# Modulations of a two-block network: fused multiply-and-sum on VectorE for all columns, none as products on TensorE

## The chip, the cores and the metric

The kernel runs on one core of a Trainium2 chip. The time is the device time of one execution in microseconds (us), lower is better. A core has TensorE (PE, the matrix engine, with its weight loads shown apart as PEld), VectorE (DVE), ScalarE (ACT), GpSimd (POOL, hardly used here) and SyncE (SP, which issues the DMAs here).

## What is computed

Two blocks are applied to 256 tokens of width 1024, in float32. The first is a recurrent mixer with a feed-forward; the second has two attention layers, which also carry 256 context tokens. Every layer of the second block is steered by modulations: six vectors of 1024 for the tokens, from a condition `c`, and six for the context, from `c_ctx`.

```python
def modulation(cond, w_ada, b_ada):
    m = jax.nn.silu(cond) @ w_ada + b_ada          # w_ada: [1024, 6144]
    return [t[..., None, :] for t in jnp.split(m, 6, axis=-1)]

def modulate(h, shift, scale):
    return h * (1 + scale) + shift

def second_block(x, c, ctx, c_ctx, w_ada, ...):
    for i in range(2):
        sh1, sc1, g1, sh2, sc2, g2 = modulation(c, w_ada[i], b_ada[i])
        csh1, csc1, cg1, csh2, csc2, cg2 = modulation(c_ctx, w_ada[i], b_ada[i])
        h = modulate(rms_norm(x, norm1_g[i]), sh1, sc1)
        ...                                        # projections, attention
        x = x + g1 * (mixed @ w_out[i])
        x = x + g2 * conv_ffn(modulate(rms_norm(x, norm2_g[i]), sh2, sc2), ...)
```

The modulations of a layer are thus two products of one row with a matrix of 1024 x 6144, and nothing of them depends on the tokens. They can be computed at any time before the layer's norms and residuals read them.

## The kernel before

Features lie on partitions, tokens along the free dimension. Every product is made from two float32r parts of each operand, a high one and a low one, in three passes (high x high, high x low, low x high; `mm3`, lines 404 to 407). A weight comes in tiles of 128 x 1024 (512 KB): `weight_raw` takes a buffer of the ring `raw` (4 buffers) and issues the DMA on SP's queue, `weight` lets ScalarE cast it to `wh` (line 383) and VectorE subtract that from the raw tile to give `wl` (line 385); both have 3 buffers. For 256 tokens one tile is 24 matmuls of 256 columns. 419 such tiles are used, besides those of the modulations. The matmuls of the last pass over a product wait for `wl`.

The program is written as Python generators, and a scheduler puts each engine's instructions into one fixed order when the kernel is compiled; an engine runs its list in that order, each instruction waiting for the semaphores it needs.

The modulations are filler work. `Ada.steps` is a generator; `ada_tick` is called after each weight tile and takes a step from it every `pace` ticks (`Knobs.pace0` to `pace3` for the stages), `ada_steps(n)` takes n steps, and `ada_rest` takes all that are left. Results go to `mods[layer]`, [128, 48, 2]: 48 blocks of 128 features for two conditions.

There are two forms of such a step:

- `ada_pe` (lines 523 to 558), on TensorE. 512 columns are four weight tiles, each cast and subtracted as any other, and per tile four matmuls of 512 columns with the conditions as the stationary operand (lines 541, 542). The sums stand on 4 partitions; two ScalarE copies, four transposes (line 528) and two VectorE sums bring them onto 128 partitions.
- `ada_dve` (lines 571 to 582), on VectorE. A transposed tile of 128 columns by 1024 rows, float32, goes through one fused instruction for each condition (line 580): multiply by the condition's row, sum along the free dimension, scale, add the bias. Such a step is one instruction and a short read of the accumulator. `ada_rows` (line 560) puts silu of the conditions on all partitions first (eight tanh, eight instructions of line 568). The tiles have a pool of their own, `araw`, with 3 buffers.

Layer 0's modulations are all made by `ada_pe(0)`, 48 tiles, from the first block's middle up to its feed-forward (called ffn1 below). Layer 1's first 5120 columns are made by `ada_dve(1)` in layer 0's feed-forward, 40 tiles and 80 steps, and the last 1024 by `ada_pe(1)`, 8 tiles, during layer 1's attention.

A feed-forward (`ffn`) runs over chunks of the hidden width: the up-projection (per hidden block two weights, a short convolution with four tap instructions on VectorE, SwiGLU, a split), then eight down products, each added to the residual stream `xres` on VectorE (line 1316 in ffn1, line 1641 in the second block). ffn1 has two such chunks, of 14 and 8 blocks. After the last one come the sums of squares (`sacc`, lines 471 and 473), a reduction of them on PE (`psn`), and the next norm; at the same time PE goes on with the next layer's first weights (`psx`, lines 429 to 431), which serve the context's tokens first.

Of the kernel before, what the change touches and what calls it, by code (L numbers as in the profile page):

```python
# [28 lines left out]
# columns of the modulations done on the tensor engine, 512 at a time, and on the vector engine, 128  # L29
ADA = ((range(0, 6144, 512), range(0)), (range(5120, 6144, 512), range(0, 5120, 128)))  # L30
# [3 lines left out]
# column offsets of the first block's w_in  # L34
# [4 lines left out]
# rows of the small projections: i gates, f gates, dt  # L39
# [3 lines left out]
def _ws(name, layer, c0, nk=8, r0=0):  # L43
    """[nk*128, 128] block of a weight, rows on partitions, 128 columns."""
    def cut(w):
        return w[name][layer][r0:r0 + nk * 128, c0:c0 + 128].reshape(nk, 128, 128).transpose(1, 0, 2)
    return nk * 128, cut


def _xs(name, layer, c0, half, cols=None):  # L50
    """[512, 256] block: rows on partitions, 256 columns that stream."""
    def cut(w):
        a = w[name][layer][half * 512:(half + 1) * 512]
        a = a[:, c0:c0 + 256] if cols is None else a[:, cols]
        return a.reshape(4, 128, 256).transpose(1, 0, 2)
    return 1024, cut


def _ada(layer, c0, q):
    """[256, 512] block: rows on partitions, 512 columns."""  # L60
    def cut(w):
        a = w["w_ada_2"][layer][q * 256:(q + 1) * 256, c0:c0 + 512]
        return a.reshape(2, 128, 512).transpose(1, 0, 2)
    return 1024, cut


def _adat(layer, c0):
    """[1024, 128] block: columns on partitions."""
    def cut(w):
        return w["w_ada_2"][layer][:, c0:c0 + 128].T  # L70
    return 1024, cut
# [16 lines left out]
def _qcols(c):  # L88
    """256 columns of the window attention's queries, heads j and j + 4 side by side."""
# [35 lines left out]
def plan2(layer):  # L125
    p = [(("ada", c0, q), _ada(layer, c0, q)) for c0 in ADA[layer][0] for q in range(4)]
    p += [(("adat", c0), _adat(layer, c0)) for c0 in ADA[layer][1]]
# [21 lines left out]
def _cols(v):  # L149
    """[n*128] -> [128, n]"""  # L150
    return v.reshape(-1, 128).T


def _convc(w):
    """[K, n*128] -> [128, n*K]"""
# [121 lines left out]
class Knobs:  # L277
# [4 lines left out]
    araw = 3  # L282
# [3 lines left out]
    pace3 = 5  # L286
# [3 lines left out]
    afill = tuple(range(20, 30))  # L290
# [9 lines left out]
def tile_two_blocks(ctx: ExitStack, tc: tile.TileContext, xT, ctxT, cst1, cst, cstw, pb1, pl0, pl1, pf0, pf1, pc, pcb, wb, w0, w1, out,  # L300
# [16 lines left out]
    class PS:  # L317
        """PSUM pools of the phase at hand"""

    def psum(**bufs):  # L320
        """Shares out the eight banks: name=number."""
# [7 lines left out]
    psum(g=3, s=4, a=1)  # L329
# [30 lines left out]
    ones = const.tile([128, 128], F32, name="ones")  # L360
    V.memset(ones, 1.0)
    onesn = const.tile([128, 128], F32, name="onesn")
# [5 lines left out]
    def bsel(r):  # L368
        """[128, 128]: row r ones; picks and broadcasts one row."""
        return ident[:, r:r + 1].to_broadcast([128, 128])  # L370

# [21 lines left out]
    def gained(dst_h, dst_l, x, g):  # L393
        """x g, split: what the first products after a norm take; 1 / rms is applied to their results"""
# [4 lines left out]
    def mm3(o, w, rhs, nk, late=False, first=True, last=True):  # L399
        """o = W^T x in three passes; late: the low part of x comes last."""  # L400
# [11 lines left out]
    def gemm_ws(ph, key, rhs, n, nk=8, late=False, w=None):  # L412
        """out[128 features, n tokens] = W^T x; rhs(k) gives (high, low)."""
# [6 lines left out]
    def gemm_xs(ph, keys, lhs, toks, evac):  # L420
        """out[128 tokens, 256 features]; lhs(k, t) gives (high, low) of a token tile."""
# [14 lines left out]
    def rsqrt_raw(pool, a, n, tag, bufs, rows=128):  # L436
        """RS * result = 1 / sqrt(a)"""
# [3 lines left out]
        # in two halves, so that neither waits for the step before  # L441
# [13 lines left out]
    def mean_sq(x, scale=None, eps=EPS):  # L455
        """mean of squares + eps, [128 tokens, 2 blocks of them], in PSUM"""
# [20 lines left out]
    def rms_all(a):  # L477
        """[128, 256] on every partition: 1 / (RS sqrt(a)) for tokens on partitions"""
# [19 lines left out]
    # =====================================================================  # L498
    # modulation: silu(c) w + b for both conditions, features on partitions
    # =====================================================================  # L500
    mods = [res.tile([128, 48, 2], F32, name="mod%d" % i) for i in range(2)]

    class Ada:
        pool = rows = None
# [5 lines left out]
    def ada_prep():  # L510
        zp = ctx.enter_context(tc.tile_pool(name="zp", bufs=1))
        Ada.cs = zp.tile([128, 8, 2], F32, name="ccs")
        Ada.cr = zp.tile([128, 8, 4], F32R, name="ccr")
        ct2 = zp.tile([128, 8, 2], F32, name="ct2")
        nc.sync.dma_start(out=ct2.rearrange("p k c -> p (k c)"), in_=pc)
        Ada.pf = [load_params(zp, _pf(i), (pf0, pf1)[i], "pf%d" % i) for i in range(2)]
        th = zp.tile([128, 8, 2], F32, name="cth")
        S.activation(out=th, in_=ct2, func=AF.Tanh, scale=0.5)
        V.scalar_tensor_tensor(th, th, 1.0, ct2, ALU.add, ALU.mult)
        V.tensor_scalar(Ada.cs, th, 0.5, None, ALU.mult)  # L520
        split(Ada.cr[:, :, 0:2], Ada.cr[:, :, 2:4], Ada.cs)

    def ada_pe(li):
        """512 columns at a time on the tensor engine; both parts of the conditions share a pass."""
        def finish(c0, rows):
            pt = PS.s.tile([128, 4, 4], F32, tag="s", name="psat")
            for q in range(4):
                T.transpose(pt[:, q], rows[q // 2][0:4, q % 2 * 128:q % 2 * 128 + 128], ident[0:4, 0:4])
            o = slice(c0 // 128, c0 // 128 + 4)
            V.tensor_tensor(mods[li][:, o], pt[:, :, 0:2],  # L530
                            Ada.pf[li]("bada")[:, o].unsqueeze(2).to_broadcast([128, 4, 2]), ALU.add)
            V.tensor_tensor(mods[li][:, o], mods[li][:, o], pt[:, :, 2:4], ALU.add)

        last = None
        for c0 in ADA[li][0]:
            ps = (PS.a or PS.s).tile([128, 512], F32, tag="s", name="psada")
            for q in range(4):
                wh, wl = weight(1 + li, ("ada", c0, q), 512)
                for kk in range(2):
                    k = 2 * q + kk  # L540
                    T.matmul(ps[0:4], Ada.cr[:, k], wh[:, kk], start=(k == 0), stop=False)
                    T.matmul(ps[0:2], Ada.cr[:, k, 0:2], wl[:, kk], start=False, stop=(k == 7))
                if last and q == 0:
                    finish(*last)
                if q < 3:
                    yield
            rows = [Ada.rows.tile([128, 256], F32, tag="arow", name="arow", bufs=2) if Ada.rows is not None else
                    tmp.tile([128, 256], F32, tag="t256", name="arow", bufs=6) for _ in range(2)]
            for e in range(2):
                S.copy(rows[e][0:4], ps[0:4, e * 256:(e + 1) * 256])  # L550
            last = (c0, rows)
            if Ada.rows is None:
                finish(*last)
                last = None
            yield
        if last:
            finish(*last)
            yield
# [1210 lines left out]
```

## Time and profile before

| | |
|---|---|
| median of 3 runs | 1763.69 us (1762.58 to 1768.16) |
| span of the profiled execution | 1767.7 us |
| PE busy | 1738.8 us, 98% |
| VectorE busy | 1384.8 us, 78% |
| ScalarE busy | 983.7 us, 56% |
| DMA | 276.97 MB, mean 157 GB/s |

The profile is that of one execution; its span is 4.0 us above the median of the runs. PE, VectorE and the others have one list of instructions each. A row's first time is its start, the second its length; an instruction may overlap the one before it on the same engine, so the cost of one in a row of them is read from start to start. "Idle before" is the time in which the engine stood still before an instruction, with what released it. The granted clock (PEclk) is the share of TensorE's full clock that it ran at.

### The profile page before, as it was taken

How to read it: one execution, taken by the hardware profiler on the slowest of the kernel's cores; microseconds unless marked ns; L12 is line 12 of the kernel's file. 1: busy time of each engine (PE TensorE's matmuls, PEld its weight loads, DVE VectorE, ACT ScalarE, POOL GpSimd, SP SyncE). 2: the span in 40 equal slices, each digit the busy share in tenths (PEclk: the TensorE clock that was granted, in tenths of full speed). 3: DMA queues.
4: the chain of work that ended last, by engine and by line, in shares of the span. 5: the costliest groups of instructions: out<-in, count | busy, mean ns of one | idle time of the engine just before them, and what ended most of it. 6: DMA issues, size and time to landing. Idle time of an engine off the chain costs nothing.

```text
span 1767.7 us, 31912 instructions
## 1 busy us (share of the span) xinstructions
PE 1738.8 (98%) x12442; PEld 1568.2 (89%) x12442; DVE 1384.8 (78%) x2716; ACT 983.7 (56%) x1723; POOL 0.2 (0%) x4
## 2 busy tenths in 40 slices
PE   7999999999999999999999999999999999999999
PEld 7999988878888999999878898888888997799999
DVE  7987967557778996877687799999656878788776
ACT  6655645445556865666676564442244556766554
POOL 0000000000000000000000000000000000000000
PEclk8999999999999999999989999999999999999999
DMA  7555445447677666654211356657433543046564
GB/s 233 159 154 152 138 132 157 147 126 222 218 228 228 187 190 221 209 170 139 86 67 47 105 163 189 183 171 232 129 96 107 168 132 120 24 141 195 174 196 132
DMA packets 80502, 276.97 MB, mean 157 GB/s; under 512 B 9056, under 2 KB 13792, under 8 KB 80224
## 3 DMA queue, kind: packets, MB, share of 16 engines
q1 hardware_dynamic: 80352, 274.94, 49.8%
q8 instruction: 98, 1.61, 0.4%
q14 instruction: 52, 0.43, 0.1%
HBM read 273.86 MB, written 1.05 MB: 156 GB/s over the span
## 4 chain that ended last, share of the span: by engine, by line
PE 51%; DVE 3%; ACT 1%; issue 0%; ACTq 0%
PE psg L404 12%; PE psg L407 12%; PE psg L406 11%; PE pso L1574 3%; PE psx L429 2%; PE psx L431 2%; PE psx L430 2%; PE psp L1562 2%; PE psc L1517 1%; PE psc L1519 1%; PE psc L1518 1%; DVE wl L385 0%; ACT Pp L1529 0%; DVE mx L1523 0%; PE psc L1521 0%
## 5 line engine op out<-in xcount | busy, mean ns | idle before, releaser
L383 ACT CAST wh<-raw 128x1024 fp32r<-128x1024 f32 (+1 forms) x475 | 490.9, 1037 | 531.0 <-PE psg L406 423.7
L385 DVE TENSOR_TENSOR wl<-raw,wh 128x1024 fp32r<-128x1024 f32 (+1 forms) x475 | 572.5, 1208 | 206.8 <-ACT wh L383 203.2
L404 PE MATMUL psg<-XH,wh 128*128 128x256 f32 (+1 forms) x1288 | 400.7, 314 | 3.6 <-ACT XH L390 1.9
L407 PE MATMUL psg<-XH,wl 128*128 128x256 f32 (+1 forms) x1288 | 398.8, 312 | 0.3 <-DVE wl L385 0.3
L406 PE MATMUL psg<-XL,wh 128*128 128x256 f32 (+1 forms) x1240 | 387.5, 313 | 0.7 <-DVE XL L1304 0.5
L404 PEld LDWEIGHTS psg<-XH,wh 128*128 128x128 f32 x1288 | 243.0, 189 | 22.0 <-ACT XH L390 2.3
L407 PEld LDWEIGHTS psg<-XH,wl 128*128 128x128 f32 x1288 | 243.3, 189 | 15.9 <-DVE wl L385 1.0
L406 PEld LDWEIGHTS psg<-XL,wh 128*128 128x128 f32 x1240 | 234.5, 189 | 16.1 <-DVE XL L1304 1.1
L404 PE MATMUL psg<-xh,wh 128*128 128x256 f32 x704 | 203.4, 289 | 1.8 <-ACT xh L390 1.3
L406 PE MATMUL psg<-xl,wh 128*128 128x256 f32 x704 | 200.5, 285 | 0.9 <-DVE xl L391 0.9
L407 PE MATMUL psg<-xh,wl 128*128 128x256 f32 x704 | 200.1, 284 | 0.3 <-DVE wl L385 0.3
L404 PE MATMUL psg<-hh,wh 128*128 128x256 f32 (+1 forms) x592 | 179.6, 305 | 0.1
L407 PE MATMUL psg<-hh,wl 128*128 128x256 f32 (+1 forms) x592 | 178.5, 302 | 0.0
L406 PE MATMUL psg<-hl,wh 128*128 128x256 f32 (+1 forms) x592 | 178.5, 302 | 0.0
L404 PEld LDWEIGHTS psg<-xh,wh 128*128 128x128 f32 x704 | 134.9, 192 | 6.0 <-ACT xh L390 1.5
L406 PEld LDWEIGHTS psg<-xl,wh 128*128 128x128 f32 x704 | 135.1, 192 | 2.9 <-DVE xl L391 1.4
L407 PEld LDWEIGHTS psg<-xh,wl 128*128 128x128 f32 x704 | 134.9, 192 | 2.2 <-issue 1.3
L406 PEld LDWEIGHTS psg<-hl,wh 128*128 128x128 f32 x592 | 111.5, 188 | 5.3 <-DVE hl L391 0.2
L404 PEld LDWEIGHTS psg<-hh,wh 128*128 128x128 f32 x592 | 110.9, 188 | 5.9 <-ACT hh L390 0.6
L407 PEld LDWEIGHTS psg<-hh,wl 128*128 128x128 f32 x592 | 111.2, 188 | 5.5
L429 PE MATMUL psx<-wh,XH 128*128 128x256 f32 x384 | 110.0, 287 | 1.1 <-DVE ss L1379 0.5
L430 PE MATMUL psx<-wh,XL 128*128 128x256 f32 x384 | 108.5, 283 | 0.0
(435 smaller groups left out, 3237.8 us busy)
## 6 DMA issues: line engine op xcount, KB each, us to landing
raw<-w SPq DMA_DIRECT2D x254, 512.0 KB, 3.7
raw<-wb SPq DMA_DIRECT2D x197, 512.0 KB, 4.3
araw<-w SPq DMA_DIRECT2D x40, 512.0 KB, 4.2
raw<-w SPq DMA_DIRECT2D x16, 384.0 KB, 3.4
raw<-wb SPq DMA_DIRECT2D x8, 384.0 KB, 3.2
xres<-xT SPq DMA_DIRECT2D x16, 128.0 KB, 3.6
plt<-pl SPq DMA_DIRECT2D x2, 588.0 KB, 5.5
xres<-ctxT SPq DMA_DIRECT2D x8, 128.0 KB, 2.7
```

Source lines behind the costliest of these rows:

```text
L383: S.copy(wh[:, 0:sz], raw[:, 0:sz])
L385: V.tensor_tensor(wl[:, 0:sz], raw[:, 0:sz], wh[:, 0:sz], ALU.subtract)
L404: T.matmul(o, wh[:, k], xh, start=(first and k == 0), stop=False)
L406: T.matmul(o, wh[:, k], xl, start=False, stop=False)
L407: T.matmul(o, wl[:, k], xh, start=False, stop=(last and not late and k == nk - 1))
L429: T.matmul(o, xh, wh[:, k % 4], start=(k == 0), stop=False)
L430: T.matmul(o, xl, wh[:, k % 4], start=False, stop=False)
L431: T.matmul(o, xh, wl[:, k % 4], start=False, stop=(k == 7))
L1517: T.matmul(o, qh, kh, start=True, stop=False)
L1518: T.matmul(o, qh, kl, start=False, stop=False)
L1562: T.transpose(ps[:, b], p[:, b * 128:(b + 1) * 128], ident)
L1574: T.matmul(po[:, i % 4], pt[:, b], v, start=(b == 0), stop=(b == nb - 1))
```

## The change

All 48 tiles of both layers become `ada_dve` steps, 96 for each layer; `ada_pe` goes, and with it the conditions' split, its small DMA, the transposes and the filler list `afill`.

```diff
-ADA = ((range(0, 6144, 512), range(0)), (range(5120, 6144, 512), range(0, 5120, 128)))
+ADA = range(0, 6144, 128)
...
-    p = [(("ada", c0, q), _ada(layer, c0, q)) for c0 in ADA[layer][0] for q in range(4)]
-    p += [(("adat", c0), _adat(layer, c0)) for c0 in ADA[layer][1]]
+    p = [(("adat", c0), _adat(layer, c0)) for c0 in ADA]
...
-    araw = 3
     pace0 = 1000
     pace1 = 2
     pace2 = 1
-    pace3 = 5
+    pace3 = 2
...
-    afill = tuple(range(20, 30))
...
-    psum(g=3, s=4, a=1)
+    psum(g=3, s=5)
...
     def ada_dve(li):
-        for c0 in ADA[li][1]:
-            o, sz = woff[1 + li][("adat", c0)]
+        for c0 in ADA:
             f = c0 // 128
-            raw = Ada.pool.tile([128, 1024], F32, tag="araw", name="araw", bufs=Knobs.araw)
-            nc.sync.dma_start(out=raw, in_=wsrc[1 + li][o:o + 128 * sz].rearrange("(p f) -> p f", p=128))
+            raw = weight_raw(1 + li, ("adat", c0))
             for c in range(2):
-                to = Ada.pool.tile([128, 1024], F32, tag="prod", name="prod", bufs=1) if c == 0 else raw
+                to = Ada.pool.tile([128, 1024], BF16, tag="prod", name="prod", bufs=1) if c == 0 else raw
                 V.tensor_tensor_reduce(to, raw, Ada.cb[:, c], 0.5, Ada.pf[li]("bada")[:, f:f + 1], ALU.mult, ALU.add,
                                        accum_out=mods[li][:, f, c:c + 1])
                 yield
...
-    Ada.pace, Ada.steps, Ada.rows = Knobs.pace0, ada_pe(0), p1
+    ada_rows(p1)
+    Ada.pace, Ada.steps = Knobs.pace0, ada_dve(0)
...
     def context_norm():
-        ada_steps(max(0, 17 - Ada.done))
+        ada_steps(max(0, 32 - Ada.done))
...
-            psum(c=Knobs.c1, o=1, s=6 - Knobs.c1, a=1)
-            Ada.steps, Ada.rows = ada_pe(1), None
-            for i, _ in enumerate(seq(gmlp(0), attention((1, 0)))):
-                if i in Knobs.afill:
-                    ada_steps(1)
-            ada_rest()
+            psum(c=Knobs.c1, o=1, s=7 - Knobs.c1)
+            for _ in seq(gmlp(0), attention((1, 0))):
+                pass
```

The tiles now come through the ring of the weights, `raw`, in place of `araw`, and the discarded product of the first condition is written as BF16 in place of float32. The conditions' rows on all partitions are made twice, at the kernel's start and in layer 0's feed-forward. The pace in ffn1 goes from a step every fifth weight to one every second. Two constants of ones shrink from 128 columns to one. The rest of the diff is comments.

With 96 steps per layer and these paces, `ada_rest` at the end of ffn1 takes 26 steps and the one at the end of layer 0's feed-forward 23. The listings below show an engine's compiled instructions in turn; a fused step is a row "ISA" with `ccb` among its inputs, followed by the accumulator's row.

VectorE at the end of ffn1, before: `xres` are the residuals of the last down products, `wl_9537`, `wl_9543` and `wl_9603` the first weights of the next layer.

```order
L385 TENSOR_TENSOR wl_9356<-raw_9352,wh_9354 128x1024
L473 TENSOR_TENSOR sacc_9404<-sacc_9400,sq_9402 128x256
L1316 TENSOR_TENSOR xres_6258<-psg_9287,xres_6258 128x256
L385 TENSOR_TENSOR wl_9537<-raw_9533,wh_9535 128x1024
L473 TENSOR_TENSOR sacc_9408<-sacc_9404,sq_9406 128x256
L1316 TENSOR_TENSOR xres_6258<-psg_9319,xres_6258 128x256
L385 TENSOR_TENSOR wl_9543<-raw_9539,wh_9541 128x1024
L473 TENSOR_TENSOR sacc_9412<-sacc_9408,sq_9410 128x256
L1316 TENSOR_TENSOR xres_6258<-psg_9351,xres_6258 128x256
L385 TENSOR_TENSOR wl_9603<-raw_9599,wh_9601 128x1024
```

The same place after the change, from the last down weight on (`wl_8920`):

```order
L374 TENSOR_TENSOR wl_8920<-raw_8916,wh_8918 128x1024
L520 ISA prod_8949,mod0_90<-raw_8947,ccb_572,pf0_568 128x1024
L520 ISA mod0_90 128x1
L1257 TENSOR_TENSOR xres_5942<-psg_8850,xres_5942 128x256
L520 ISA raw_8947,mod0_90<-raw_8947,ccb_572,pf0_568 128x1024
L520 ISA mod0_90 128x1
L520 ISA prod_8954,mod0_90<-raw_8952,ccb_572,pf0_568 128x1024
L520 ISA mod0_90 128x1
L1257 TENSOR_TENSOR xres_5942<-psg_8882,xres_5942 128x256
```

It goes on in that way through 13 tiles, `raw_8947` to `raw_9007`, and ends with:

```order
L520 ISA prod_9009,mod0_90<-raw_9007,ccb_572,pf0_568 128x1024
L520 ISA mod0_90 128x1
L462 TENSOR_TENSOR sacc_9074<-sacc_9070,sq_9072 128x256
L520 ISA raw_9007,mod0_90<-raw_9007,ccb_572,pf0_568 128x1024
L520 ISA mod0_90 128x1
L1286 COPY sa_9082<-psn_9016 128x2
L1320 MEMSET ss_9154 128x104
L1288 SCALAR_TENSOR_TENSOR s3_9084<-sa_9082,psn_9049 128x2
L374 TENSOR_TENSOR wl_9165<-raw_9161,wh_9163 128x1024
```

26 steps stand between the last down weight's `wl_8920` and the next weight's `wl_9165`, with the residuals and ten sums of squares among them.

PE at the same place after the change, behind the last down product: `psx_9173` is the next layer's first product, `psn` are the reductions.

```order
L454 MATMUL psn_9016<-onesn_85,sq_9043 128x1
L418 MATMUL psx_9173<-wh_9163,XH_6320 128x256
L419 MATMUL psx_9173<-wh_9163,XL_6321 128x256
L418 MATMUL psx_9200<-wh_9163,XH_6320 128x256
L419 MATMUL psx_9200<-wh_9163,XL_6321 128x256
L454 MATMUL psn_9049<-onesn_85,sacc_9074 128x1
L454 MATMUL psn_9049<-onesn_85,sq_9076 128x1
L454 MATMUL psn_9049<-onesn_85,sacc_9074 128x1
L454 MATMUL psn_9049<-onesn_85,sq_9076 128x1
L420 MATMUL psx_9173<-wl_9165,XH_6320 128x256
```

Four products that need only `wh` stand before the reduction of `sacc_9074` and the first product with `wl_9165`.

VectorE at the end of layer 0's feed-forward, before, around the last residuals (line 1641):

```order
L385 TENSOR_TENSOR wl_15989<-raw_15985,wh_15987 128x1024
L473 TENSOR_TENSOR sacc_15915<-sacc_15911,sq_15913 128x256
L473 TENSOR_TENSOR sacc_15919<-sacc_15915,sq_15917 128x256
L1641 SCALAR_TENSOR_TENSOR xres_6669<-psg_15809,mod0_93,xres_6669 128x256
L473 TENSOR_TENSOR sacc_15923<-sacc_15919,sq_15921 128x256
L385 TENSOR_TENSOR wl_15995<-raw_15991,wh_15993 128x1024
L473 TENSOR_TENSOR sacc_15927<-sacc_15923,sq_15925 128x256
L1641 SCALAR_TENSOR_TENSOR xres_6669<-psg_15846,mod0_93,xres_6669 128x256
L1379 MEMSET ss_15970 128x104
L385 TENSOR_TENSOR wl_16061<-raw_16057,wh_16059 128x1024
```

And after the change, the last residual there and what follows it:

```order
L1582 SCALAR_TENSOR_TENSOR xres_6311<-psg_15474,mod0_90,xres_6311 128x256
L1245 SCALAR_TENSOR_TENSOR XL_6321<-h_15510,mod1_91,XH_6320 128x256
L520 ISA prod_15517,mod1_91<-raw_15515,ccb_12467,pf1_570 128x1024
L520 ISA mod1_91 128x1
L460 SCALAR_TENSOR_TENSOR sacc_15575<-sq_15571,sq_15573 128x256
L520 ISA raw_15515,mod1_91<-raw_15515,ccb_12467,pf1_570 128x1024
L520 ISA mod1_91 128x1
L520 ISA prod_15522,mod1_91<-raw_15520,ccb_12467,pf1_570 128x1024
L520 ISA mod1_91 128x1
```

Here 11 tiles, `raw_15515` to `raw_15565`, follow the last residual, and layer 1's first weight (`wl_15657`) stands behind 21 of their 22 steps.

## Rows read from the trace of the kernel before

**Rows 1.** The page's first part: busy time, share of the span and instructions per engine.

```profile
span 1767.7 us, 31912 instructions
PE 1738.8 (98%) x12442; PEld 1568.2 (89%) x12442; DVE 1384.8 (78%) x2716; ACT 983.7 (56%) x1723; POOL 0.2 (0%) x4
```

**Rows 2.** Costliest groups: line, engine, tiles, count | busy, mean ns | idle before, releaser.

```profile
L383 ACT CAST wh<-raw 128x1024 fp32r<-128x1024 f32 (+1 forms) x475 | 490.9, 1037 | 531.0 <-PE psg L406 423.7
L385 DVE TENSOR_TENSOR wl<-raw,wh 128x1024 fp32r<-128x1024 f32 (+1 forms) x475 | 572.5, 1208 | 206.8 <-ACT wh L383 203.2
```

**Rows 3.** Timeline of PE around one modulation tile: start us, length us.

```profile
433.02 0.28 PE L407 MATMUL psg<-xh,wl 128*128 128x256 f32 x1
433.14 0.39 PE L541 MATMUL psada<-wh,ccr 128*4 128x512 f32 x1
...
434.07 0.28 PE L404 MATMUL psg<-yh,wh 128*128 128x256 f32 x1
434.19 0.28 PE L406 MATMUL psg<-yl,wh 128*128 128x256 f32 x1
```

**Rows 4.** Line 541 in three stretches: busy us and count on PE and PEld.

```profile
240.00:560.00 320.00, 28.42 (x72) 6.13 (x72) 0.99 0.58 181
560.00:790.00 230.00, 9.49 (x24) 2.02 (x24) 1.00 0.62 194
1470.00:1550.00 80.00, 6.61 (x16) 1.37 (x16) 1.00 0.21 67
```

**Rows 5.** Lines 528, 580, 568, 577 one by one: ns min/median/max, first and last start.

```profile
L528 PE MATMUL psat<-ct,arow x56: 197/198/223, 299.4 to 1545.1; 4*128 4x4 f32 x56
  issue: 4.4, 10
L580 DVE CUSTOM_DVE_ANT_0 prod<-araw,ccb,pf x40: 1273/1278/1283, 1045.4 to 1251.0; 128x1024 f32<-128x1024 f32 x40
L568 DVE SCALAR_TENSOR_TENSOR ccb<-th,ccb x8: 421/422/424, 1041.9 to 1045.1; 128x256 f32<-128x256 f32 x8
DMA to landing us min/median/max: 3.3/4.2/6.4
```

**Rows 6.** Timeline of VectorE in layer 0's feed-forward, three steps in a row.

```profile
1245.37 1.28 DVE L580 CUSTOM_DVE_ANT_0 araw<-araw,ccb,pf 128x1024 f32<-128x1024 f32 x1
1246.57 0.08 DVE L580 DVE_READ_ACCUMULATOR2_ANT mod<- 128x1 f32 x1
...
1249.11 0.08 DVE L580 DVE_READ_ACCUMULATOR2_ANT mod<- 128x1 f32 x1
```

**Rows 7.** Windows: busy us of PE, PEld, DVE, ACT, POOL; granted clock, DMA share, GB/s.

```profile
580.00:650.00 70.00, 69.84 (x565) 66.39 (x565) 65.75 (x140) 52.41 (x89) 0.00 (x0) 1.00 0.67 202
695.00:742.00 47.00, 47.00 (x388) 45.45 (x387) 38.69 (x58) 29.74 (x46) 0.00 (x0) 1.00 0.67 214
1050.00:1250.00 200.00, 200.00 (x862) 161.74 (x861) 194.01 (x287) 72.07 (x93) 0.00 (x0) 1.00 0.63 194
1400.00:1410.00 10.00, 9.45 (x81) 9.39 (x81) 7.34 (x18) 3.79 (x8) 0.00 (x0) 1.00 0.62 197
1470.00:1545.00 75.00, 74.08 (x488) 52.57 (x486) 56.11 (x153) 54.92 (x118) 0.00 (x0) 1.00 0.19 58
```

**Rows 8.** Timeline of VectorE in the last down products of ffn1.

```profile
764.32 0.42 DVE L1316 TENSOR_TENSOR xres<-psg,xres 128x256 f32<-128x256 f32 x1 [0.23 <-PE psg L407]
765.33 1.23 DVE L385 TENSOR_TENSOR wl<-raw,wh 128x1024 fp32r<-128x1024 f32 x1 [0.58 <-ACT wh L383]
766.47 0.42 DVE L473 TENSOR_TENSOR sacc<-sacc,sq 128x256 f32<-128x256 f32 x1
767.12 0.42 DVE L1316 TENSOR_TENSOR xres<-psg,xres 128x256 f32<-128x256 f32 x1 [0.23 <-PE psg L407]
```

**Rows 9.** Windows around waits of PE, columns as in rows 7.

```profile
900.00:915.00 15.00, 13.49 (x66) 11.37 (x65) 12.68 (x39) 12.02 (x27) 0.00 (x0) 0.66 0.19 61
927.00:932.00 5.00, 5.00 (x20) 3.56 (x18) 3.71 (x15) 3.23 (x6) 0.00 (x0) 0.66 0.00 0
```

More of the change, by code (lines that the diff above doesn't have):

```diff
@@ L55, in cut @@
         return a.reshape(4, 128, 256).transpose(1, 0, 2)
[L56 to L63, printed above, removed]
     return 1024, cut
@@ L359, in tile_two_blocks @@
     ident = C("ident")
-    ones = const.tile([128, 128], F32, name="ones")
+    ones = const.tile([128, 1], F32, name="ones")
     V.memset(ones, 1.0)
-    onesn = const.tile([128, 128], F32, name="onesn")
+    onesn = const.tile([128, 1], F32, name="onesn")
     V.memset(onesn, 1.0 / 1024.0)
@@ L503, in tile_two_blocks @@
     class Ada:
-        pool = rows = None
         ticks = 0
@@ L511, in ada_prep @@
         zp = ctx.enter_context(tc.tile_pool(name="zp", bufs=1))
[L512 to L515, printed above, removed]
         Ada.pf = [load_params(zp, _pf(i), (pf0, pf1)[i], "pf%d" % i) for i in range(2)]
-        th = zp.tile([128, 8, 2], F32, name="cth")
-        S.activation(out=th, in_=ct2, func=AF.Tanh, scale=0.5)
@@ L519, in ada_prep @@
[L519 to L558, printed above, removed]
@@ L560, in ada_rows @@
     def ada_rows(pool):
-        t = pool.tile([128, 2, 1024], F32, name="ccb")
-        v = t.rearrange("p c k -> p (c k)")
+        Ada.pool = pool
+        Ada.cb = pool.tile([128, 2, 1024], F32, name="ccb")
+        v = Ada.cb.rearrange("p c k -> p (c k)")
         nc.sync.dma_start(out=v, in_=pcb)
@@ L568, in ada_rows @@
             V.scalar_tensor_tensor(v[:, i:i + 256], th, 1.0, v[:, i:i + 256], ALU.add, ALU.mult)
-        return t
     def ada_dve(li):
-        for c0 in ADA[li][1]:
-            o, sz = woff[1 + li][("adat", c0)]
+        for c0 in ADA:
             f = c0 // 128
-            raw = Ada.pool.tile([128, 1024], F32, tag="araw", name="araw", bufs=Knobs.araw)
-            nc.sync.dma_start(out=raw, in_=wsrc[1 + li][o:o + 128 * sz].rearrange("(p f) -> p f", p=128))
+            raw = weight_raw(1 + li, ("adat", c0))
             for c in range(2):
-                to = Ada.pool.tile([128, 1024], F32, tag="prod", name="prod", bufs=1) if c == 0 else raw
+                to = Ada.pool.tile([128, 1024], BF16, tag="prod", name="prod", bufs=1) if c == 0 else raw
                 V.tensor_tensor_reduce(to, raw, Ada.cb[:, c], 0.5, Ada.pf[li]("bada")[:, f:f + 1], ALU.mult, ALU.add,
@@ L1672, in layer @@
             run_ratio(seq(units(("av", "au"), 0), units(("cv",), 0, 1)), seq(qk_part(0), qk_part(1)), Knobs.rc)
-            psum(c=Knobs.c1, o=1, s=6 - Knobs.c1, a=1)
-            Ada.steps, Ada.rows = ada_pe(1), None
-            for i, _ in enumerate(seq(gmlp(0), attention((1, 0)))):
-                if i in Knobs.afill:
-                    ada_steps(1)
-            ada_rest()
+            psum(c=Knobs.c1, o=1, s=7 - Knobs.c1)
+            for _ in seq(gmlp(0), attention((1, 0))):
+                pass
         at.close()
@@ L1713, in layer @@
             zs = ExitStack()
-            Ada.pool = zs.enter_context(tc.tile_pool(name="zq", bufs=1))
-            Ada.cb = ada_rows(Ada.pool)
+            ada_rows(zs.enter_context(tc.tile_pool(name="zq", bufs=1)))
             Ada.pace, Ada.steps = Knobs.pace2, ada_dve(1)
```

## The prediction

> **What bounds the kernel now.** I read the busy shares first: TensorE (PE) is busy 98% of the span, VectorE (DVE) 78%, ScalarE (ACT) 56% [rows 1]. A busy PE alone does not prove that PE sets the end, so the costliest groups come second: the casts of the weights wait 423.7 us in sum for PE to give buffers back, and the subtractions wait 203.2 us for the casts [rows 2]. Work queues up behind PE, hence a product taken off PE is time saved, as long as VectorE keeps delivering low parts `wl`. Third come the windows, since 78% is a mean: VectorE is busy 65.75 of 70 us in the first feed-forward's up-projection, 38.69 of 47 in its second one, 194.01 of 200 in layer 0's feed-forward, while PE is at 100% or nearly so [rows 7]. There is room on VectorE, but not at every place. The change gives PE less and VectorE more, so what counts is where.
>
> **What is taken off PE.** A modulation tile costs PE four matmuls of 512 columns. They stand between 433.14 and 434.07, so 0.93 us [rows 3]. 112 matmuls of line 541, two per tile, make 56 tiles: 36 (72 matmuls) before the first feed-forward, 12 (24) in it, 8 (16) in layer 1's attention [rows 4]. 56 x 0.93 = 52 us. With them go 56 transposes, which lasted 0.20 us each but overlap other work, and for which PE sat idle 4.4 us in ten places [rows 5]; I take 4 us, between 0 and 11. Together **-56 us** (52 to 63). ScalarE loses 56 casts and the row copies; it was not the bound, so that is worth nothing by itself.
>
> **What is put on VectorE.** 112 more fused instructions (192 instead of 80) for 56 subtractions and 28 small sums fewer. One lasts 1.278 us and three of them, each with its read of the accumulator, went from 1245.37 to 1249.11, so 1.25 us a step [rows 5, 6]. That is 112 x 1.25 = 140 us more, 56 x 1.21 = 68 us less [rows 2]. The product's copy is written as BF16 now, which no row shows. It can't cost more than the same pass, so 1.25 is the upper end; the lower end is half of it, 0.63, for output of half the bytes. I take 1.25, because the two sources stay float32 and the copy is as long as before.
> [...] The row says 1.278 us for 1024 elements from two float32 sources with an accumulated sum [rows 5], against 1.23 us for a plain subtraction of the same size [rows 8]. [...]
>
> **Where the steps stand.** Most follow a weight each or every second one, and PE's 2.8 us per weight (from one residual to the next [rows 8]) hide them if VectorE has 1.25 us to spare. But the pace does not bring all of them in. The compiled order has 26 steps left at the end of the first feed-forward and 23 at the end of layer 0's, in one piece, ahead of the next weights' subtractions, as the listings of the order show. VectorE works its list in order, so PE gets no new `wl` meanwhile. Before, the subtractions of the next weights stood between the last residuals, one every 2.8 us [rows 8], and PE went through (9.45 of 10 us busy at layer 0's end [rows 7]).
> First clump: let t0 be the end of the fourth-last down product's matmuls, the point that frees the last weight's buffers. That weight's subtraction ended 2.2 us after such a point before (xres at 764.32, `wl` 765.33 and 1.23 long [rows 8]); PE ends its last three products at t0 + 8.4. VectorE's list from t0 + 2.2: 26 x 1.25 = 32.5, ten sums of squares and three residuals at 0.42 = 5.5 [rows 8], the first new `wl` 1.2, so t0 + 41.4. PE has about 1 us of other matmuls. The stall is 41.4 - 8.4 - 1 = **+32 us**.
> Second clump: in the last eight products VectorE has a step per weight and the next norm beside it, so I give it no lead. After the last residual come 21 steps = 26.3, six sums at 0.42 = 2.5, some small ones 1.8, the `wl` 1.2: 31.8, less 1 of other matmuls, **+31 us**. Both could be up to 6 less if VectorE is ahead, or 4 more.
>
> **The crowded up-projection.** In 580 to 650 VectorE was busy 65.75 us and PE gets through about 23 weights and 5 modulation tiles. Take off 5 subtractions and their sums (6.5 us), add a step for every second weight (11.5 x 1.25 = 14.4): 73.6 us of VectorE against 70 - 5 x 0.93 = 65.4 of PE. VectorE sets this stretch, 8 us beyond the saved PE time. In 695 to 742: 38.69 - 3.7 + 8 x 1.25 = 45.0 against 47 - 2.8 = 44.2, so 1 more; with joints between them **+10 us** (0 to 16).
>
> **Smaller terms.** Where PE had been waiting, its clock was down for a while: the mean granted clock is 0.66 in 900 to 915, where PE missed 1.5 us, and in 927 to 932 [rows 9]. [...] Each clump makes PE wait much longer than that; I take 3 us for each, **+6** (2 to 10). The conditions' rows are prepared at the start as well: eight instructions of 0.42 us on VectorE [rows 5], eight tanh on ScalarE, 1 MB of DMA behind the first weights, **+2** (0 to 6). In layer 1's attention the 8 tiles (7.4 us) were filler while PE was busy 74.08 of 75 us [rows 7]; without them some waits on the softmax come out, **+3** (0 to 7). In all other places a step replaces a subtraction one for one and stays under PE.
>
> **Sum.** -56 + 32 + 31 + 10 + 6 + 2 + 3 = +28. On the profiled span of 1767.7 that is 1795.7; the median of the runs is 4.0 us below that span, so **1791 us**, 1.5% slower.
>
> **Rivals.**
> (a) Faster: the fused step gets cheaper with the BF16 copy. At 0.63 us the clumps shrink by 26 x 0.62 = 16 and 21 x 0.62 = 13, the up-projection no longer binds: 28 - 29 - 10 = -11, 1753 us. The point from which it decides is a step of about 0.7 us for -0.3%. For it: half the bytes written. Against: the subtraction and the fused step last alike [rows 5, 8], which points to the elements read. [...]
> (b) Faster: the clumps hide. Were the next weights' low parts ready before the steps, the sum would be -56 + 10 + 2 + 3 = -41, 1723 us; one of two hidden gives about 1757. The order speaks against it: the new `wl` is listed behind the steps.
> (c) Level: VectorE arrives early at both clumps and nothing is lost elsewhere: -56 + 26 + 25 + 2 + 2 = -1, 1763 us.
> (d) Slower still: the clumps wait for memory. Raw tiles now share a ring of four with the weights. A tile of 512 KB landed in 4.2 us, 6.4 at most [rows 5], and in a clump one is wanted every 2.5 us. With three on the way that suffices. Were only one on the way at a time, 13 x 4.2 = 55 instead of 32.5 and 11 x 4.2 = 46 instead of 26 put 42 us on top, 1833 us.
> That steps are not emitted at all is excluded: the order lists 96 for each layer.
>
> **How the numbers follow.** The forecast with its own range, 1773 to 1808: 0.66. (a) 0.06, (b) 0.07, (c) and what is near it 0.09, half of it within 0.3%; (d) 0.07; 1769 to 1773 has the rest, 0.05. A measurement of this kernel tells about 0.3% (5.3 us) from no change. Faster: 0.06 + 0.07 + 0.03 = 0.16; within: 0.07; slower: 0.77. A range of 1760 to 1812 leaves out (a), (b) and most of (d), somewhat under 0.2.
>
> **What would show it.** In the changed trace: PE idle for about 30 us around the end of the first feed-forward and again at the end of layer 0's, waiting for `wl`, with VectorE full of fused steps back to back at 1.25 us. PE's busy sum lower by some 50 us, the time up to the first feed-forward shorter by 30 to 35 us; the first feed-forward's up-projection at VectorE 100%. Wrong would be: a step under 1 us, clumps during which PE works on, DMA waits between the steps, or a first half that is no shorter.

## The result and the profile after

The changed kernel takes 1808.01 us (median of 4 runs, 1806.69 to 1815.13), the kernel before 1765.93 beside it: a ratio of 1.0235 (95% interval 1.0206 to 1.0264), 2.35% slower. The profiled span is 1805.9 us, 38.2 above the one before. The forecast was 1791 in a range of 1760 to 1812, slower at 0.77: the direction and the range held. The time came out 17 us above the forecast. Of the loss, 28 us were forecast; the profiled spans show 38 and the two medians 42.

The first part of the page, three of its rows in 40 slices and three of its costliest groups; they answer to [rows 1, 2, 5]:

```profile
span 1805.9 us, 31311 instructions
PE 1694.7 (94%) x12162; PEld 1555.6 (86%) x12162; DVE 1444.1 (80%) x2861; ACT 927.8 (51%) x1645; POOL 0.2 (0%) x4
...
PE   7999999999989899589999999999999399999999
...
DVE  8987968577889889967786998775678967689766
...
PEclk9999999999999999779989999999999798999999
...
L372 ACT CAST wh<-raw 128x1024 fp32r<-128x1024 f32 (+1 forms) x419 | 433.0, 1036 | 462.9 <-PE psg L395 309.8
L374 DVE TENSOR_TENSOR wl<-raw,wh 128x1024 fp32r<-128x1024 f32 (+1 forms) x419 | 503.9, 1206 | 106.2 <-ACT wh L372 103.9
...
L520 DVE CUSTOM_DVE_ANT_0 prod<-raw,ccb,pf 128x1024 bf16<-128x1024 f32 x96 | 123.1, 1283 | 74.5 <-DMA raw<-w 74.4
```

PE's busy sum fell by 44 us, but its share fell from 98 to 94%: it now waits. Two slices of PE stand out, a 5 and a 3, and the clock is down beside them. The fused step with its BF16 copy lasts 1.28 us as the float32 one did, so rival (a) is out.

The two dips, as windows (busy us of PE, PEld, DVE, ACT, POOL; granted clock, DMA share, GB/s): first the end of the first feed-forward (ffn1), then that of layer 0's.

```profile
740.00:750.00 10.00, 4.42 (x38) 4.21 (x36) 10.00 (x20) 2.16 (x5) 0.00 (x0) 0.91 0.69 204
750.00:760.00 10.00, 1.87 (x8) 1.78 (x8) 10.00 (x19) 2.43 (x5) 0.00 (x0) 0.50 0.65 177
760.00:770.00 10.00, 0.00 (x0) 0.00 (x0) 10.00 (x18) 0.51 (x2) 0.00 (x0) 0.50 0.67 196
770.00:780.00 10.00, 6.46 (x28) 6.08 (x29) 9.43 (x30) 3.14 (x3) 0.00 (x0) 0.50 0.75 215
...
1412.00:1442.00 30.00, 5.31 (x36) 4.82 (x34) 30.00 (x58) 3.69 (x10) 0.00 (x0) 0.64 0.65 200
```

VectorE is full and PE nearly idle: the two clumps, where they were forecast. At the first one PE reads like this (start, length, idle before and its releaser):

```profile
756.87 0.59 PE L454 MATMUL psn<-onesn,sacc 128*128 128x1 f32 x2 [12.46 <-DVE sacc L462]
...
771.75 0.58 PE L418 MATMUL psx<-wh,XH 128*128 128x256 f32 x1 [13.01 <-ACT wh L372]
...
776.62 0.58 PE L420 MATMUL psx<-wl,XH 128*128 128x256 f32 x1 [1.40 <-DVE wl L374]
```

And ScalarE and VectorE there, two of the 26 steps and the first new weight:

```profile
768.93 1.28 DVE L520 CUSTOM_DVE_ANT_0 prod<-raw,ccb,pf 128x1024 bf16<-128x1024 f32 x1
770.13 0.09 DVE L520 DVE_READ_ACCUMULATOR2_ANT mod<- 128x1 f32 x1
770.13 0.42 DVE L462 TENSOR_TENSOR sacc<-sacc,sq 128x256 f32<-128x256 f32 x1
770.47 1.28 DVE L520 CUSTOM_DVE_ANT_0 raw<-raw,ccb,pf 128x1024 f32<-128x1024 f32 x1
...
770.65 1.04 ACT L372 CAST wh<-raw 128x1024 fp32r<-128x1024 f32 x1 [10.14 <-DMA raw<-w]
...
775.26 0.16 DVE L1288 SCALAR_TENSOR_TENSOR s<-sa,psn 128x2 f32<-128x2 f32 x1 [0.45 <-PE psn L454]
775.34 1.23 DVE L374 TENSOR_TENSOR wl<-raw,wh 128x1024 fp32r<-128x1024 f32 x1
```

The reductions `psn` wait for sums of squares spread between the steps, and the next product waits even for its high part: ScalarE stood 10.14 us for the weight's DMA. The new weight comes through the same ring as 13 step tiles, and gets a buffer only when the steps have freed one. So the clump held the weight's load as well as its subtraction. The steps themselves did not wait for the ring, as rival (d) has it: they run back to back, and from the last down weight's subtraction to 775.34 VectorE stands still for 0.45 us alone. The late load therefore decided what PE waited for, hardly how long: the low part comes last, and it comes when VectorE's list reaches it.

To place the rest of the time, I read from the traces when each weight's subtraction starts (line 374, before line 385), over the 419 weights besides the modulations, and took differences at eight places. The columns are the profiled executions of the kernel before, of the changed one, and of the experiments told below; us. Each column is one execution. In the first row e1 and e3, whose code is alike up to there, differ by 5 us (234.1 and 229.0), so a difference of that size in one cell shows nothing by itself.

| stretch | before | after | e1 | e2 | e3 | e4 | e5 | e9 | e10 |
|---|---|---|---|---|---|---|---|---|---|
| first block, 64 weights (changed kernel: 2 steps at its end; e10: 20) | 228.8 | 230.6 | 234.1 | 231.2 | 229.0 | 227.9 | 231.4 | 232.2 | 235.3 |
| from there to ffn1 | 322.9 | 287.3 | 295.7 | 289.1 | 297.0 | 282.6 | 283.7 | 288.2 | 297.8 |
| ffn1 up to its last weight | 204.8 | 213.5 | 206.2 | 215.4 | 203.8 | 192.7 | 193.1 | 216.7 | 197.4 |
| four weights on, the first clump | 15.0 | 52.2 | 13.5 | 51.2 | 13.3 | 15.0 | 91.7 | 51.0 | 15.0 |
| layer 0 up to its feed-forward | 269.8 | 265.3 | 265.7 | 266.8 | 266.8 | 266.8 | 262.6 | 263.6 | 270.1 |
| that, with the second clump | 378.1 | 411.8 | 411.4 | 388.5 | 384.7 | 373.7 | 415.7 | 372.8 | 373.2 |
| layer 1's attention | 170.7 | 169.9 | 168.0 | 167.8 | 170.4 | 169.3 | 168.4 | 169.5 | 169.0 |
| rest | 160.6 | 158.4 | 158.4 | 158.8 | 158.5 | 156.7 | 156.7 | 156.7 | 156.4 |

After less before: 34 us gained up to ffn1, 9 lost in it, 37 lost at the first clump, 4 gained in layer 0, 34 lost around the second, 1 and 2 gained behind: +38.

### The profile page after: what moved, and what is told of

Its sections match the earlier page's. It is cut to its first block, busy times and chain, and to the rows that moved or that the text cites. A ratio compares the mean times of both kernels' runs of the same rounds, so it can differ in the third digit from the quotient of the medians.

```text
span 1805.9 us, 31311 instructions
## 1 busy us (share of the span) xinstructions
PE 1694.7 (94%) x12162; PEld 1555.6 (86%) x12162; DVE 1444.1 (80%) x2861; ACT 927.8 (51%) x1645; POOL 0.2 (0%) x4
## 4 chain that ended last, share of the span: by engine, by line
PE 73%; DVE 15%; DMA 6%; issue 3%; ACT 3%; SPq 0%; ACTq 0%; DVEq 0%
PE psg L393 16%; PE psg L396 16%; PE psg L395 16%; DVE wl L374 4%; PE psx L420 3%; PE psx L418 3%; DMA raw<-w 3%; PE psx L419 3%; PE pso L1515 3%; DMA raw<-wb 2%; DVE prod L520 2%; PE psp L1503 2%; ACT wh L372 2%; PE psc L1458 1%; DVE raw L520 1%
## 5 line engine op out<-in xcount | busy, mean ns | idle before, releaser
L372 ACT CAST wh<-raw 128x1024 fp32r<-128x1024 f32 (+1 forms) x419 | 433.0, 1036 | 462.9 <-PE psg L395 309.8
L374 DVE TENSOR_TENSOR wl<-raw,wh 128x1024 fp32r<-128x1024 f32 (+1 forms) x419 | 503.9, 1206 | 106.2 <-ACT wh L372 103.9
L520 DVE CUSTOM_DVE_ANT_0 prod<-raw,ccb,pf 128x1024 bf16<-128x1024 f32 x96 | 123.1, 1283 | 74.5 <-DMA raw<-w 74.4
L520 DVE CUSTOM_DVE_ANT_0 raw<-raw,ccb,pf 128x1024 f32<-128x1024 f32 x96 | 122.8, 1279 | 0.1
```

The costliest lines, as they stand in the source:

```text
L372: S.copy(wh[:, 0:sz], raw[:, 0:sz])
L374: V.tensor_tensor(wl[:, 0:sz], raw[:, 0:sz], wh[:, 0:sz], ALU.subtract)
L520: V.tensor_tensor_reduce(to, raw, Ada.cb[:, c], 0.5, Ada.pf[li]("bada")[:, f:f + 1], ALU.mult, ALU.add, accum_out=mods[li][:, f, c:c + 1])
```

## Experiments

Each ran beside the kernel before on the same chip, whose medians there were 1766.1 to 1768.3.

| kernel | median us | ratio to before | 95% interval |
|---|---|---|---|
| after | 1808.0 | 1.0235 | 1.0206 to 1.0264 |
| e1_l0_even | 1770.8 | 1.0018 | 1.0003 to 1.0033 |
| e2_l1_even | 1784.0 | 1.0088 | 1.0070 to 1.0105 |
| e3_both_even | 1744.0 | 0.9856 | 0.9830 to 0.9881 |
| e4_no_steps | 1705.9 | 0.9645 | 0.9631 to 0.9659 |
| e5_double_clump | 1826.3 | 1.0330 | 1.0311 to 1.0348 |
| e6_filler_kept | 1743.1 | 0.9858 | 0.9843 to 0.9873 |
| e7_start_early | 1742.1 | 0.9863 | 0.9839 to 0.9888 |
| e8_no_filler | 1767.7 | 1.0005 | 0.9995 to 1.0014 |
| e9_own_ring_l1 | 1767.4 | 0.9994 | 0.9980 to 1.0008 |
| e10_own_ring | 1728.8 | 0.9771 | 0.9747 to 0.9795 |

**Are the clumps paid at their place?** Three kernels pace the same steps so that none is left over, first for layer 0, then for layer 1, then for both.

```diff
-    pace1 = 2
+    pace1 = 1
     pace2 = 1
-    pace3 = 2
+    pace3 = 3
```

> The changed kernel with other paces for layer 0: a step after every weight before the first feed-forward (instead of every second) and every third weight in it, so that no step is left at its end. Theory A (the clump of 26 steps is paid at its place, 37 us in the changed kernel from the last down weight to the third weight behind it): 1808 less 37 for the clump, less 5 to 8 for the lighter up-projection (15 steps instead of 22), plus up to 4 in the stretch before, where VectorE was 70 to 82% busy and takes 34 steps more: 1762 to 1774, and PE idle no longer than 5 us at the end of the first feed-forward. Theory B (VectorE's or the ring's sum of work sets the time, and the clump is only where it shows): the steps cost the same elsewhere, 1795 or more.

Measured 1770.8: 39 us below the changed kernel (1.0235 x 1768.3 = 1809.8). The stretch behind the last weight is back at 13.5 us, and ffn1 is 7 us shorter with 24 steps instead of 32 (counted in the traces between the weights that bound the stretch). What the steps cost more lies before ffn1: 8 us for 34 more of them.

```diff
             def hook(j):
+                ada_steps(2 if j == 0 else 1)
                 if j == 16:
```

> The changed kernel with one more step after each hidden block of layer 0's feed-forward, so that none of layer 1's steps is left at its end (one of 23 remains). Theory A: 33 us less than the changed kernel, 1770 to 1780; PE stays at 100% in the up-projection, where VectorE has 173 of 230 us busy and gets 30 us more. Theory B: the steps cost the same elsewhere, 1795 or more.

Measured 1784.0: 26 us less, against 33 expected. The clump is gone, but seven steps still stand among the last eight down products, and the stretch keeps 388.5 where e4, without steps, has 373.7.

> Both of the above at once. Theory A: the two add, 1728 to 1745, faster than the kernel before by 1 to 2%. Theory B: 1785 or more. If the two clumps hid each other's cost (a third reading: VectorE behind after the first one makes the second longer), e3 would gain less than e1 and e2 together, by 10 us or more.

Measured 1744.0, faster than the kernel before by 1.4%. 66 us less than the changed kernel, and e1 and e2 give 39 + 26 = 65: they add. Theory B and the third reading are out. The count of steps and the work on VectorE are the same in all four kernels; where the steps stand moves the time by up to 66 us.

**What do the modulations cost on TensorE?** e4 leaves out all modulation work; the modulations are the bias alone.

```diff
     def ada_dve(li):
-        for c0 in ADA:
-            ...
+        for c in range(2):
+            V.tensor_copy(mods[li][:, :, c], Ada.pf[li]("bada"))
+            yield
```

> Leaves out all modulation work: no tiles are loaded, no fused steps, no rows of the conditions; the modulations are the bias alone. The time is that of everything else, so the kernel before minus this one is what the modulations cost there, in all. Theory A (PE was the bound, and a tile costs its 0.93 us): 1766 less 52 to 60, 1706 to 1714, plus up to 7 if PE's clock falls in layer 1's attention without filler, as it did in the changed kernel from 1519 to 1533. Rival C (much of the products on PE lay in waits that stay): 1725 or more.

Measured 1705.9, 62 us below the kernel before. The 62 hold everything that the modulations cost there, the 80 steps on VectorE too (the stretch with them is 4.4 us longer than in e4). By place: from the first step to ffn1 40.3 us for 36 tiles, 1.12 each where the matmuls alone show 0.93. In ffn1 12.1 us for 12. But layer 1's attention lost only 1.4 us with its 8 tiles. That is 53.8 for the 56 tiles, near the 56 of the forecast, but otherwise shared out.

**Does a clump grow with its steps?** e5 doubles it: no steps in ffn1.

```diff
-    pace3 = 2
+    pace3 = 1000
```

> The changed kernel without steps in the first feed-forward, so that 59 instead of 26 are left at its end. Theory A (a clump costs its steps one by one, and the crowded up-projection costs what the run without any modulation work lacks): the stretch from the first up weight to the fourth-last down weight falls from 213 to 193 to 197 us, the one behind it rises from 52 by 33 x 1.25 = 41 to about 93; in sum 18 to 27 us slower than the changed kernel, 1826 to 1836. Theory B (steps cost the same wherever they stand): 1808 again, within 6 us.

Measured 1826.3, some 19 us slower than the changed kernel, at the low end of the 18 to 27. ffn1 (the row that ends at its last weight, which the expectation calls the fourth-last down weight) fell to 193.1 us, the stretch behind it rose from 52.2 to 91.7, 39.5 more for 32 steps more (one of the 59 runs a weight earlier), 1.23 each. Two rows of VectorE in e5, the last down weight's subtraction and the next weight's, with 58 steps between them:

```profile
714.36 1.22 DVE L374 TENSOR_TENSOR wl<-raw,wh 128x1024 fp32r<-128x1024 f32 x1
...
797.30 1.22 DVE L374 TENSOR_TENSOR wl<-raw,wh 128x1024 fp32r<-128x1024 f32 x1
```

They stand 82.9 us apart. Much the same steps cost 20.4 us inside ffn1 (30 of them) and 39.5 in the clump (32).

**Was the filler in layer 1's attention worth taking off PE?** e8 is the kernel before without it, e6 and e7 are e3 with it put back (built on the kernel before, with the steps' code of the changed one).

```diff
             for i, _ in enumerate(seq(gmlp(0), attention((1, 0)))):
-                if i in Knobs.afill:
-                    ada_steps(1)
-            ada_rest()
+                pass
```

> The kernel before, leaving out the 8 modulation tiles of layer 1's attention (their 1024 columns get the bias alone). Theory D (filler is free there): within 2 us of the kernel before, with PE's granted clock at its lower level for 10 us or more between 1470 and 1550. Theory E: 8 x 0.93 = 7.4 us faster, 0.4%, and the clock stays up.

Measured 1767.7, ratio 1.0005 (0.9995 to 1.0014): taking 8 x 0.93 us off PE gave nothing, and layer 1's attention takes 172.8 us in e8 against 170.7 before. The window that the kernel before spends at full clock with PE busy 74.08 of 75 us [rows 7] reads in e8, first in whole and then its slow part:

```profile
1470.00:1545.00 75.00, 71.42 (x421) 52.59 (x422) 44.12 (x135) 44.10 (x102) 0.00 (x0) 0.89 0.05 15
...
1472.00:1492.00 20.00, 18.80 (x62) 12.04 (x63) 7.36 (x21) 8.33 (x19) 0.00 (x0) 0.57 0.09 31
```

PE waits some 2.7 us more, then its granted clock falls: 0.57 on the mean of 20 us. With 0.50 as the lower level, which the clumps show (750 to 780 of the changed kernel), that is some 17 us of it, an estimate. The changed kernel does the same:

```profile
1515.00:1535.00 20.00, 17.36 (x58) 10.78 (x59) 8.75 (x24) 8.64 (x20) 0.00 (x0) 0.66 0.16 53
```

The clock reads 0.50 there from 1521 to 1533. The mean of 0.66 is 13.6 us at that level, so 6.8 lost, an estimate, about the 7.4 saved. That the clock alone takes the gain is argued from these rows; whether waits for the softmax would have taken it at full clock too was not separated.

> The evenly paced kernel (e3_both_even), but the last 8 tiles of layer 1 go back to TensorE as filler in its attention, as in the kernel before; the 80 other steps then end before the last eight down products. Theory D (in that attention the filler is free: it only keeps PE busy, whose clock otherwise falls, and takes no time of its own): attention stays at 168 to 171 us, the crowded end of layer 0's feed-forward falls by 6 to 9 us from e3's 43, in all 1735 to 1739. Theory E (PE bounds the attention too, so 8 x 0.93 = 7.4 us come back): attention 176 to 178, in all 1742 to 1745.

Measured 1743.1, outside the 1735 to 1739 of theory D; the sum alone would fit theory E. The places decide, and they came out as theory D says: the attention 170.9 us with the filler against 170.4 without, and the part from layer 0's last eight down products on (49.0 against 56.5 in e3) is shorter by 7.5. But layer 0's stretch, which the edit doesn't aim at, was 4.9 us longer than in e3 and ffn1 1.9. The kernel is built from the other source, so its order differs elsewhere too. In layer 0's stretch all four kernels of that source take 268 to 272 us (before, e6, e7, e8), and all of the changed source but e10 take 263 to 267; why stays open. With that in it, the filler kept on PE shows no gain in the whole time: 1743.1 against e3's 1744.0.

> e6_filler_kept with 12 of layer 0's steps started in the first 64 weights, where VectorE was 85% busy; none is left behind the first chunk of the first feed-forward. Theory A (a step costs nothing where VectorE has room, and up to its 1.25 us where it has none): 3 to 5 us saved from the 181st to the 204th weight, 0 to 5 paid in the first 64, so within 4 us of e6. If those 12 cost their full 15 us, VectorE is the bound there already, 1745 or more.

Measured 1742.1, within 1 us of e6: ffn1 6 us shorter, the first stretch 2.7 longer. Steps move for about what they save, once the clumps are gone.

**What makes the clumps?** In the kernel before, layer 1's 80 steps met only 73 ticks (the changed kernel's 96 less the 23 left over, at the same pace), yet none was left over: in its compiled order they all stand early in the feed-forward. Their tiles had a pool of their own. e9 gives layer 1 that pool back and changes nothing else.

```diff
-            raw = weight_raw(1 + li, ("adat", c0))
+            if li == 0:
+                raw = weight_raw(1 + li, ("adat", c0))
+            else:
+                o, sz = woff[1 + li][("adat", c0)]
+                raw = Ada.pool.tile([128, 1024], F32, tag="araw", name="araw", bufs=Knobs.araw)
+                nc.sync.dma_start(out=raw, in_=wsrc[1 + li][o:o + 128 * sz].rearrange("(p f) -> p f", p=128))
```

> The changed kernel with one part undone: layer 1's tiles come through a pool of their own again (3 buffers), paces and calls as changed. In the compiled order the steps then run ahead of their place in the program: all 96 stand before the 301st weight, none is left behind the feed-forward. Theory F (the shared ring is what ties the steps to their place and so makes the clump): the stretch from the 254th to the 335th weight falls from 412 to 378 to 384 us, in all 28 to 34 less than the changed kernel, 1774 to 1781. Rival (the ring doesn't matter, the number of steps does): 1800 or more, since 96 steps in the first 46 weights crowd VectorE there as the clump did behind them.

Measured 1767.4, 42 us less than the changed kernel, more than was expected, and level with the one before. The feed-forward with what follows takes 372.8 us with 96 steps in it, and 373.7 in e4 without any (373.2 in e10, with 96): there they are free, the last eight down products included, which the expectation had not counted. Two windows of e9, the stretch with the steps and the place where the second clump was:

```profile
1050.00:1250.00 200.00, 200.00 (x910) 164.87 (x910) 195.81 (x296) 78.06 (x108) 0.00 (x0) 1.00 0.59 187
...
1390.00:1410.00 20.00, 20.00 (x173) 19.89 (x172) 19.36 (x38) 13.35 (x23) 0.00 (x0) 1.00 0.57 180
```

VectorE is at 98% and PE at 100% for 200 us: nearly all of the room is used and nothing lost.

e10 does the same for layer 0. Its pool has one buffer, and the weights' ring gives it.

```diff
-    raw = 4
+    raw = 3
+    araw = (1, 3)
...
-            raw = weight_raw(1 + li, ("adat", c0))
+            o, sz = woff[1 + li][("adat", c0)]
+            raw = Ada.pool.tile([128, 1024], F32, tag="araw", name="araw", bufs=Knobs.araw[li])
+            nc.sync.dma_start(out=raw, in_=wsrc[1 + li][o:o + 128 * sz].rearrange("(p f) -> p f", p=128))
```

> As e9_own_ring_l1, and layer 0's tiles through a pool of their own too, of one buffer, for which the weights' ring gives one (3 instead of 4). In the compiled order 81 of layer 0's steps then stand before the first feed-forward, 15 in its first chunk, none behind it. Theory F: a further 37 less for the first clump and 10 to 15 less in the first feed-forward, up to 8 more in the stretch before, where VectorE gets 44 steps more: 1725 to 1740. If three buffers are too few for the weights' transfers, or one for the tiles', PE or VectorE would wait for DMA and the time would be 1745 or more.

Measured 1728.8, 2.3% faster than the kernel before and 4.5% faster than the changed one (0.9771 / 1.0235 = 0.955), the best of all. Its page, and the wait of the steps for their tiles:

```profile
PE 1683.5 (97%) x12162; PEld 1545.2 (89%) x12162; DVE 1442.6 (83%) x2861; ACT 928.0 (54%) x1645; POOL 0.2 (0%) x4
...
L523 DVE CUSTOM_DVE_ANT_0 prod<-araw,ccb,pf 128x1024 bf16<-128x1024 f32 x96 | 122.9, 1280 | 26.4 <-DMA araw<-w 26.2
```

Both clumps are gone with the changed paces left as they are. PE's busy sum is 11 us under the changed kernel's, the time 79. One buffer for layer 0's tiles and three for the weights were enough for that; VectorE waits 26 us for tiles, where the changed kernel waited 74. The steps before ffn1 are not free there: the first two stretches take 22.6 us more than in e4, for 82 steps. So the number of steps is not what makes this change slow. It takes both, the shared ring and paces that leave steps over: other paces with the shared ring remove the clumps (e3), and so do pools of their own with the same paces (e9, e10). With the shared ring the steps keep their place among the weights; with a pool of their own they stand far ahead of it: before the 301st weight e9 and e10 have all 96 steps of layer 1, the changed kernel 48.

## Why the prediction was right, and where its sizes were off

**Bound.** PE as the bound held: with no modulations at all the kernel is 62 us faster (e4), and what was lost at the clumps and in ffn1 is time in which PE waited or ran at its lower clock (0.50 from 750 to 780).

**The gain.** The term was -56 for 56 tiles. In their stretches they were worth 53.8 (before against e4), but the places were not alike: 1.12 us a tile up to ffn1, 1.01 in it, 0.2 in layer 1's attention. That last place is a step that failed: 7.4 us were booked with only 3 given back, though the windows had PE at full clock with the filler and no row without it. The measured net is 0.8 us.

**The clumps.** Forecast 32 and 31, with 3 each for the clock; measured 37.2 and 33.7, the clock included. For the first one the sum put the new `wl`'s end at t0 + 41.4. The residual that follows t0 started at 736.25, some 0.2 us behind it, and that `wl` ended at 776.57, so t0 + 40.5. The way PE waited was not foreseen in full: it stood 12.5 us for a sum of squares and 13.0 for `wh`, because the weight's load stood in the ring behind 13 step tiles, and only 1.4 for `wl`. As `wl` came last all the same, the sum held. No run shows the 3 us for the clock apart from the rest; they were the author's estimate. What the changed kernel's trace shows is a clock of 0.50 for another 5.4 and 4.3 us (to 782 and 1451) after PE had gone on with `wl` at 776.62 and 1446.76, with the matmuls of 256 columns 0.21 us apart, against 0.12 at full clock (700 to 703). By that some 2.4 and 1.9 us were lost, an estimate.

**The crowded up-projection.** Forecast 10 us beyond the PE time, so ffn1 about 2 us shorter than before. It came out 8.7 us longer, 20.8 above e4. This is the term that was most mis-sized. Its window of 580 to 650 summed VectorE's busy time against PE's and took the larger; but over the whole of ffn1 each step cost some part of its time, 4.7 us for 14 steps (e10), 11.1 for 24 (e3), 20.8 for 32 (after), all against e4. VectorE need not be full for that: over ffn1 it is busy 191 of 213.6 us, where the forecast expected 100% in the up-projection. In this window of the changed kernel's up-projection PE misses 2.9 us of 22 and its clock is at 0.89, while VectorE has 3.1 us left:

```profile
600.00:622.00 22.00, 19.06 (x139) 18.50 (x139) 18.92 (x44) 12.65 (x22) 0.00 (x0) 0.89 0.55 168
```

Over ffn1 (524.0 to 737.6) the waits of the changed kernel, in all, times, longest:

```profile
PE psg L396 <- DVE wl L374: 6.1, 7, 1.8
PE psg L393 <- DVE ag L565: 4.5, 3, 1.8
...
DVE prod L520 <- DMA raw<-w: 12.2, 6, 3.7
```

PE waits 18.9 us there in all, 14.5 of them for VectorE, against 2.4 in e4, and its mean clock is 0.97 against 0.99. That is 16.5 us of waits and some 5 for the clock, an estimate from the two mean clocks over 213.6 and 192.7 us, together about the 20.8. The forecast had no clock term for this place. VectorE's waits for step tiles explain little of it: 9.9 of the 12.2 us fall behind 650, where PE waits 4.8. Which steps hold up which of PE's products was not separated.

**The price of a step.** 1.25 us held: 1.23 a step in e5's clump, and the fused instruction with its BF16 copy lasts 1.28. The 16-bit copy did not shorten it: 1.283 us with it, 1.278 without [rows 5].

**Sum.** With the 4 us for the transposes shared out by tiles, the forecast's +28 and the measured +38 differ by 10.8 in ffn1, 4.2 in the attention and 1.9 at the clumps, and the other way by 6.7 in layer 0 and behind the attention, where nothing was booked. Every kernel of the source before has that time in layer 0 (268 to 272 us against 263 to 267, e10 apart) and behind the attention (159 to 161 against 156 to 159), so it goes with the source, but no run here shows its cause; that it made the sum look better than its terms is luck. The start's +2 is 1.8 in the profiles, less than the 5 us by which e1 and e3 differ there, so it is not tested. The stretch to ffn1 gained 35.6 where 36 were booked, but from other parts: the tiles were worth 40.3, and 36 steps cost 4.7 of it (after against e4). That the two meet is luck too. The right direction rests on the clumps, 70.9 us measured for 69.

**Rivals.** (a) is excluded by the step's length. (b), hidden clumps, did not happen; e10, which has no clumps, takes 1728.8, near the 1723 that was given, but by moving the steps forward. (d) did not occur inside the clumps. Its sign, DMA waits between the steps, is there elsewhere: of the 74 us that VectorE waited for step tiles, 34 lie in 1200 to 1300 of the changed kernel, where PE stayed busy, and 12 in ffn1.

## What to carry to other kernels

Filler work that goes to another engine should be costed where it will stand, not by its sum: the same 192 steps gave 1808, 1744 or 1729 us by where they stood, whether paces or pools put them there. Read the compiled order for runs of one kind of work, and look at what shares its buffers: here the pool shared between filler and the main stream tied the filler to its place in the program (48 of layer 1's steps before the 301st weight, 96 with a pool of their own) and put the main stream's load behind it (ScalarE stood 10.14 us for it). And filler on the bounding engine may give nothing when it goes, as the 7.4 us of e8 did (1.0005 of the time before); look for what that engine does without it, its clock included.

## What the runs showed of the hardware

Taking 8 tiles' matmuls out of an attention stage did not shorten it (172.8 us in e8, 170.7 before): PE's granted clock was 0.57 on the mean of 1472 to 1492 in e8, behind waits (PE busy 19.97 of 22 us from 1450 to 1472), and with the filler it had stayed at 1.00 from 1470 to 1545. The changed kernel's clock, 0.966 on the mean against 0.991, is down in both clumps as PE idles (0.50 from 750 to 780, 0.64 on the mean of 1412 to 1442). A pool of one 512 KB buffer served layer 0's steps in e10 with 26 us of waits of VectorE for tiles in all, while the shared ring of four had VectorE waiting 3.6 to 4.5 us for a tile eight times between 1210 and 1280. PE was busy for all of 1200 to 1285, so that cost nothing there.
